# The first pair group of a fused transformer trunk: sums moved into the head, five subtractions moved to GpSimd, gate loads in bursts, stores shifted by a step

## The chip, the cores and the metric

The kernel runs on one core of a Trainium2 chip. TensorE (PE in the profile) multiplies, with a separate sequence of weight loads (PEld); VectorE (DVE), ScalarE (ACT) and GpSimd (POOL) work element by element; SyncE (SP) issues nearly all transfers, in program order. The metric is the device time of one execution in microseconds. Less is better.

## The reference

One decoder layer on 2048 tokens of width 1024, in float32:

```python
mod = silu(c) @ w_ada + b_ada;  shift, scale, gate = split(mod, 3)
u = x * (1 + scale) + shift
q, k, v, a_gate, p_in, p_gate, m_a, m_p = split(u @ w_in, ...)
a = sliding_window_sink_attention(q, k, v, ...) * silu(a_gate) @ w_attn_proj
p = group_linear(multiscale_causal_pool(p_in)) * pool_scale * silu(p_gate) @ w_pool_proj
y = (sigmoid(m_a) * a + sigmoid(m_p) * p) @ w_out * (1 + gate)
x = layer_norm(alpha * x + y)
```

Attention has 16 query heads and 2 key heads of width 64, blocks of 128 and a window of 128.

## The kernel before, in words

**A quad.** The kernel computes large products with a Strassen-like scheme of seven products instead of eight. A `Quad` is two output rows of 128 by two column halves of 512. The moving operands are seven sets (B11, T1, T2, B21, T3, B22, T4), each four tiles of 128x512 in a high and a low part: every float32 operand is split into a rounded high part (a copy on ScalarE) and the rest (a subtraction on VectorE, the helper `low`), and each product runs three matmuls per tile, high x high, high x low, low x high. So one product of a quad with one set is 12 matmuls of 128x512. The weights of a quad go through four stages, F (B11, T1), S (T2, B21), Th (T3, B22) and L (T4), and each stage's weights are sums of loaded quarters: `sum1` and `mid` before F and S, `late` before Th, on GpSimd unless another engine is given. A `w_set` tile in the profile is a split weight, `set_B` and `set_T` the sets, `A` the last quarter. `behind` takes the results out: after T2 it adds the bank of T2's product and a copy of the T1 result (tile `p5`) into the quad's second accumulator, b; the accumulators then go to `consume`.

**The plan.** `plan` orders the products, the splits of weights and the loads of the next quads by steps, one step per product. `run` walks the steps; `at(step, f)` hangs a function on a step, and `defer(n, f)` runs it n steps later. Hooks of a step are emitted behind its product, deferred work behind the hooks. Each engine executes what it is given in this order, and waits only for the data and buffers that the instruction needs: an engine with an empty queue runs an instruction as soon as its inputs exist, whatever step it was written in.

**The first pair group.** The first two quads (keys and values `kv`, and queries `q` 0 and 1) are computed as a pair. Their stages F and S are done in `head`, while x, w_ada and the first weights arrive: `head` loads everything, computes shift and scale on TensorE and VectorE, modulates x, and builds B11, T1, B21, T2 and then T3 as their inputs appear. The arrays `xs` and `ts` hold the modulated input and its differences. B22 is split from `xs[4..7]`, and T4 is `xs[4..7]` minus `ts`. What is left at the end of `head` is hung on steps counted from `base`, the step of the pair's first S product: the late weights of the second quad at step 0, the split of B22 at step 3, T4's differences at step 4, T4's split at step 5. The products still to be run for the pair are, from step 4: T3, B22 of `kv`, T3, B22 of `q`, T4 of `kv`, T4 of `q`; then, at step 10, B11 of the next pair (the gates `ag` and `pg`).

**Work in between.** In the same steps `fold_parts` folds w_pool_mix into the pool's part of w_in: sixteen small products, one per step from step 6, that use the banks pv and pt in turn. Each needs a piece of weights loaded five steps before (`room_raw`, three pieces and one mix matrix), split into `room_w` two steps before, and its result is copied by ScalarE (`st`, in a ring of three tiles of tag x) and stored to `wmix_d`. `gate_modulation` computes the gate: sixteen loads of 128x512 of w_ada into `room_small`, one per step from step 6, each multiplied and summed on VectorE two steps later. `turn_v` transposes value tiles on TensorE through pt and pv, splits them into the second half of `room_small` and stores them. `keep_k` stores key tiles; `q_quad.consume` makes a query tile (`q_hi`, `q_lo`, a ring of four tiles) and stores both parts two steps later.

The steps of the prediction touch lines 235 to 290 (`Quad`), 451 to 475 (`behind`), 546 to 584 (`kv_quad`, `q_quad`), 1170 to 1190 (`gate_modulation`) and 1212 to 1431 (`head` and `first_start`). Every instruction has line 56 in the profile, that of a helper, so groups are told apart by their tiles.

Of the kernel before, what the change touches and what calls it, by code (L numbers as in the profile page):

```python
# [15 lines left out]
ALU = mybir.AluOpType  # L16
# [43 lines left out]
def kernel(  # L60
# [23 lines left out]
    pe, act, dve, pool, sp = (Ordered(tc, e) for e in (nc.tensor, nc.scalar, nc.vector, nc.gpsimd, nc.sync))  # L84
# [9 lines left out]
    def set_tile(n):  # L94
        return cp.tile([P, 4, 2, CH], F32R, tag=f"set_{n}", name=f"set_{n}")

    sets = {n: set_tile(n) for n in ("B11", "T1", "B21")}
# [16 lines left out]
    class SetStore:  # L114
        def __init__(self, name, order=SUM_ORDER):
            self.t = dp.tile([7, 4, P, CH], F32, name=name)
            self.slot = {n: i for i, n in enumerate(order)}
# [15 lines left out]
    q_d = dp.tile([2, KT, 2, 2, P, CH], F32, name="q_d")  # L133
    k_d = dp.tile([2, P, 2, D], F32, name="k_d")
# [6 lines left out]
    def cols(t, n):  # L141
        return t[:, n * CH : (n + 1) * CH]
# [4 lines left out]
    def as32(ap):  # L147
        return ap.bitcast(F32)

    def low(engine, dst, src, hi):  # L150
        engine.tensor_tensor(dst, src, as32(hi), ALU.subtract)

    def mm(*args, **kw):
        pe.matmul(*args, **kw)
# [80 lines left out]
    class Quad:  # L235
        def __init__(self, srcs, consume, sums=None, again=False):
            self.srcs, self.consume, self.sums, self.again = srcs, consume, sums, again
            self.at, self.parts, self.rings, self.opened, self.prefetch = {}, {}, {}, False, None

        def load_w(self, ph, q=sp, a12=True):  # L240
            self.w = x = ph.weights()
            if self.again:
                q.dma_start(x[:, 1:3, :], self.sums)
            else:
                q.dma_start(x[:, 2, :], self.srcs[1][:, 0:CH])
            if a12:
                q.dma_start(x[:, 0::3, :], by_two(self.srcs[0]))
            else:
                q.dma_start(x[:, 0, :], self.srcs[0][:, 0:CH])
# [63 lines left out]
    def defer(ticks, f, local=False):  # L313
        due.append((now[0] + ticks, len(due), f, local))
# [7 lines left out]
    def at(p, f):  # L322
        assert p >= now[0], (p, now[0])
        hooks.setdefault(int(p), []).append(f)
# [126 lines left out]
    def behind(ph, q, kind, h):  # L451
        if kind == "F":
            if h == 0:
                q.c = bank(("lg", "c1")[q.x] if q.pair else "mm")
                if q.x and ph.fresh:
                    t = sets["B11"][:, 0, 0, :]
                    mm(q.c, t[:, 0:P], t, start=True, stop=True, skip_group_check=True)
                    ph.fresh = False
                act.copy(q.c, q.a)
            else:  # L460
                q.p5 = ph.p("p5")
                act.copy(q.p5, q.b)
        elif kind == "S":
            if h == 0:
                dve.tensor_tensor(q.b, q.c, q.p5, ALU.add)
            else:
                q.consume(ph, 0, 0, q.a)
        elif kind == "Th":
            if h == 0:
                dve.tensor_tensor(q.p5, q.c, q.p5, ALU.add)  # L470
                q.consume(ph, 1, 1, q.p5)
            else:
                q.consume(ph, 0, 1, q.b)
        else:
            q.consume(ph, 1, 0, q.c)
# [70 lines left out]
    def kv_quad(s):  # L546
        def keep_k(ph, t, src):
            hi, lo = ph.pair()
            act.copy(hi, src)
            low(dve, lo, src, hi)  # L550
            defer(2, lambda: [sp.dma_start(cols(k_d[s, :, n, :], t), as32(x)) for n, x in enumerate((hi, lo))])

        def turn_v(ph, t, vt):
            vtp = bank(("pv", "pt")[t]).rearrange("p (b a d) -> p b a d", b=NB, a=2)
            for b in range(NB):
                pe.transpose(vtp[:, b].rearrange("p a d -> p (a d)"), vt[:, b * P : (b + 1) * P], ident)
            v = ph.two_halves()
            hi, lo = (v.rearrange("p (a b n d) -> p n b a d", a=2, b=NB, n=2)[:, n] for n in range(2))
            act.copy(hi, vtp)
            low(dve, lo, vtp, hi)  # L560
            v = as32(v).rearrange("p (a b d) -> p a b d", a=2, b=NB)
            defer(2, lambda: [sp.dma_start(v_d[s, :, a, NB * t : NB * (t + 1)], v[:, a]) for a in range(2)])

        def consume(ph, mi, t, src):
            if mi == 0:
                keep_k(ph, t, src)
            else:
                vt = ph.own("vt") if s == 0 else cols(ph.spare(), 0)
                act.activation(vt, src, AF.Copy, scale=0.5)
                defer(2, lambda: turn_v(ph, t, vt))  # L570

        return Quad((win[TK], win[TV]), consume)

    def q_quad(s, m):
        def consume(ph, mi, t, src):
            hi, lo = ph.c("q_hi", F32R), ph.c("q_lo", F32R)
            act.activation(hi, src, AF.Copy, scale=-0.125)
            dve.scalar_tensor_tensor(lo, src, -0.125, as32(hi), ALU.mult, ALU.subtract)
            defer(2, lambda: [sp.dma_start(q_d[s, m + mi, t, n], as32(x)) for n, x in enumerate((hi, lo))])

        kept = (sums_d[1 + m // 2], s == 1) if m else ()
        return Quad((win[TQ + m], win[TQ + m + 1]), consume, *kept)
# [517 lines left out]
    rooms = {}  # L1100
# [69 lines left out]
    def gate_modulation(base):  # L1170

        def room(j):
            return cols(rooms["small"], j % 2)

        def fetch(j):
            sp.dma_start(room(j), cols(wada[2 * KT + j // 2], j % 2))

        def work(j):
            m = mod[:, 2 * KT + j // 2 : 2 * KT + j // 2 + 1]
            w = room(j)  # L1180
            dve.tensor_tensor_reduce(w, w, cols(rooms["cb"], j % 2), 1.0, m, ALU.mult, ALU.add, m)

        def gate_row():
            dve.tensor_scalar(mod[:, 2 * KT :], mod[:, 2 * KT :], 0.5, None, ALU.mult)

        for j in range(2 * KT):
            p = base + 6 + j
            at(p, lambda j=j: fetch(j))
            at(p + 2, lambda j=j: work(j))
        at(base + 24, gate_row)  # L1190
# [21 lines left out]
    def head(ph, grp):  # L1212
# [6 lines left out]
        small = ph.t.tile([P, 2 * D], F32, tag="small", bufs=1, name="head_small")  # L1219
# [21 lines left out]
        xs, ts, sums, starts = {}, {}, {}, []  # L1241
# [33 lines left out]
        def minus(dst, a, b):  # L1275
            dve.tensor_tensor(dst, a, b, ALU.subtract)

        def parts(name, i, src):
            split_set(name, i, src, (act, dve))
# [30 lines left out]
        opened = [[bank(), bank(), None, None] for q in grp]  # L1310
# [80 lines left out]
        sets["T3"] = set_tile("T3")  # L1391
        for i in range(4):
            parts("T3", i, xs[i][0])
        third = [ph.split(False) for _ in range(2)]
        act.copy(by_two(third[0]), grp[0].third())
        low(dve, by_two(third[1]), grp[0].third(), by_two(third[0]))
        grp[0].parts["Th"] = third

        def t4_sums():
            for i in range(4):  # L1400
                minus(xs[4 + i][0], xs[4 + i][0], ts[i])
            sets["T4"] = set_tile("T4")

        def late_parts(name, c):
            return lambda: [parts(name, i, xs[4 + i][c]) for i in range(4)]

        sets["B22"] = set_tile("B22")
        dve.tensor_scalar(nsink, nsink, -1.0, None, ALU.mult)
        rest = (0, lambda: grp[1].late(dve)), (3, late_parts("B22", 1)), (4, t4_sums), (5, late_parts("T4", 0))
        for q, o in zip(grp, opened):  # L1410
            q.a, q.b, q.c, _, q.p5 = o
            q.opened = True
        return rest

    def first_start(ph, phase):
        rest = head(ph, phase["groups"][0])
        base = phase["base"]
        rooms["raw"] = ph.t.tile([P, 2 * D], F32, tag="big", bufs=1, name="room_raw")
        rooms["w"] = ph.t.tile([P, 2 * D], F32R, tag="big2", bufs=1, name="room_w")

        def small_room():
            rooms["small"] = ph.t.tile([P, 2 * D], F32, tag="small", bufs=1, name="room_small")

        ph.turns["v"] = cycle([lambda: cols2(rooms["small"], 1).bitcast(F32R)])
        for n, f in rest:
            at(base + n, f)
        at(base + 5, small_room)
        for j in range(2):
            at(base + 10 + j, lambda j=j: spread_bias(j, act))
        fold_parts(ph, base)  # L1430
        gate_modulation(base)
# [73 lines left out]
    parts = []  # L1505
# [61 lines left out]
```

## Time and profile before

| | |
|---|---|
| time, median of 3 runs | 1728.42 us (1728.2 to 1731.76) |
| the profiled execution: time, span, mean granted clock | 1734.96 us, 1732.8 us, 0.986 |
| busy PE, DVE, ACT, POOL | 1675.2, 1273.3, 945.2, 588.6 us |
| chain that ended last | PE 68%, DVE 11%, DMA 8%, ACT 7%, issue 5% |
| DMA | 389.50 MB, 225 GB/s |

A time below is in microseconds from the start of the span. In the timeline each row is a start, a duration, the engine, the operation with its output and inputs, and in brackets how long the engine had been idle before and what ended that. `SPq` is SyncE's issue of a transfer; its duration is the time the issue took, with waiting. `xN` stands for N instructions merged into a row.

### The profile page before, as it was taken

What the parts mean: (1) busy time and instruction counts of PE and PEld (TensorE: products, weight loads), DVE (VectorE), ACT (ScalarE), POOL (GpSimd) and SP (SyncE); (2) the same over time, 40 slices, a digit from 0 to 9 for tenths busy, and PEclk for the clock granted to TensorE, in tenths of its full rate; (3) what the DMA queues carried; (4) which work ended last, traced back from release to release, by engine and by line L of the source; (5) the groups of instructions that cost most, each with busy time, mean ns of one, the idle gap of its engine ahead of it and who ended that gap; (6) DMA issues with size and microseconds to landing.
All of it is one profiled execution on the core that took longest, in us unless ns stands there. A gap on an engine that the chain in (4) does not pass through costs nothing.

```text
span 1732.8 us, 24858 instructions
## 1 busy us (share of the span) xinstructions
PE 1675.2 (97%) x8112; PEld 1399.7 (81%) x8112; DVE 1273.3 (73%) x2296; ACT 945.2 (55%) x1815; POOL 588.6 (34%) x562
## 2 busy tenths in 40 slices
PE   9889999999999999999999999999999999999996
PEld 7678788878788888888888888888788888888775
DVE  5846787768757778558787887587877785877667
ACT  3644777667753445457767677334544343435442
POOL 3012455545453223323424333322232211124443
PEclk8999999989999999999999999999999999999998
DMA  9389666766556788864446453689968786785432
GB/s 352 123 280 295 216 221 223 253 211 192 186 174 218 258 284 307 296 223 150 152 167 211 152 187 124 199 282 310 341 212 292 237 316 215 239 292 200 146 146 109
DMA packets 236545, 389.50 MB, mean 225 GB/s; under 512 B 20840, under 2 KB 90240, under 8 KB 236288
## 3 DMA queue, kind: packets, MB, share of 16 engines
q1 hardware_dynamic: 235344, 386.55, 66.4%
q8 instruction: 64, 1.05, 0.3%
q10 hardware_dynamic: 1040, 1.34, 0.2%
q14 instruction: 65, 0.53, 0.1%
q0 software_dynamic: 32, 0.02, 0.0%
HBM read 243.63 MB, written 147.35 MB: 226 GB/s over the span
## 4 chain that ended last, share of the span: by engine, by line
PE 68%; DVE 11%; DMA 8%; ACT 7%; issue 5%; SPq 1%; POOL 0%; DVEq 0%; ACTq 0%; POOLq 0%
PE mm L56 42%; PE lg L56 11%; PE c L56 9%; DVE w_set L56 3%; PE pv L56 3%; PE pt L56 3%; DVE wide L56 2%; DVE L L56 2%; ACT L L56 2%; ACT w_set L56 2%; SPq L56 1%; DMA q_d<-q_hi 1%; ACT sig L56 1%; DMA out_dram<-wide 1%; DMA bt<-e_rep 1%
## 5 line engine op out<-in xcount | busy, mean ns | idle before, releaser
L56 PE MATMUL mm<-set_B,w_set 128*128 128x512 f32 x2664 | 656.0, 393 | 1.4 <-DVE w_set L56 1.2
L56 PEld LDWEIGHTS mm<-set_B,w_set 128*128 128x128 f32 x2664 | 499.5, 189 | 104.9 <-DVE w_set L56 1.7
L56 POOL TENSOR_TENSOR W<-W 128x512 f32<-128x512 f32 x185 | 270.0, 1469 | 579.4 <-DVE w_set L56 380.1
L56 PE MATMUL mm<-set_T,w_set 128*128 128x512 f32 x1824 | 453.1, 396 | 0.5 <-DVE set_T L56 0.5
L56 PEld LDWEIGHTS mm<-set_T,w_set 128*128 128x128 f32 x1824 | 341.2, 190 | 70.6 <-DVE set_T L56 1.6
L56 DVE TENSOR_TENSOR w_set<-W,w_set 128x1024 fp32r<-128x1024 f32 x198 | 256.1, 1294 | 121.1 <-ACT w_set L56 111.2
L56 ACT CAST w_set<-W 128x1024 fp32r<-128x1024 f32 x222 | 232.2, 1047 | 85.4 <-PE mm L56 48.8
L56 ACT ACTIVATE L<-L 128x257 f32<-128x257 f32 (+3 forms) x384 | 191.2, 500 | 117.9 <-DVE L L56 117.2
L56 PE MATMUL c<-set_T,w_set 128*128 128x512 f32 x864 | 212.5, 394 | 5.5 <-ACT w_set L56 3.0
L56 PE MATMUL lg<-set_T,w_set 128*128 128x512 f32 x864 | 211.0, 392 | 4.8 <-DVE mm L56 1.6
L56 PEld LDWEIGHTS c<-set_T,w_set 128*128 128x128 f32 x864 | 162.8, 190 | 42.0 <-ACT w_set L56 4.2
L56 PEld LDWEIGHTS lg<-set_T,w_set 128*128 128x128 f32 x864 | 161.6, 188 | 41.7 <-DVE set_T L56 2.8
L56 POOL TENSOR_TENSOR W<-W,A 128x512 f32<-128x512 f32 x41 | 56.0, 1365 | 275.5 <-DMA A<-in_win_dram 130.5
L56 DVE CUSTOM_DVE_ANT_0 L<-lg,bt,nsink 128x256 f32<-128x256 f32 (+1 forms) x256 | 111.0, 470 | 23.3 <-PE lg L56 16.8
L56 DVE TENSOR_TENSOR ptl<-pt,pth 128x512 fp32r<-128x512 f32 (+1 forms) x128 | 85.8, 670 | 29.9 <-ACT pth L56 29.0
L56 PEld LDWEIGHTS lg<-kk,qs 128*128 128x128 f32 x512 | 76.5, 190 | 37.1 <-DVE L L56 27.0
L56 PE MATMUL lg<-kk,qs 128*128 128x256 f32 (+1 forms) x512 | 83.6, 286 | 18.6 <-DVE L L56 18.5
L56 DVE TENSOR_SCALAR L<-L 128x256 f32<-128x256 f32 (+1 forms) x128 | 96.6, 755 | 4.5
L56 ACT ACTIVATE sig<-mm 128x512 f32<-128x512 f32 x76 | 45.5, 598 | 96.9 <-PE mm L56 94.7
L56 ACT CAST pth<-pt 128x512 fp32r<-128x512 f32 (+1 forms) x128 | 72.2, 564 | 23.8 <-PE pv L56 23.0
L56 PE MATMUL pv<-pth,vv 128*128 128x256 f32 x248 | 75.6, 326 | 2.1 <-DMA vv<-v_d 2.1
L56 POOL TENSOR_TENSOR w_set<-W,w_set 128x1024 fp32r<-128x1024 f32 x24 | 58.1, 2422 | 56.8 <-ACT w_set L56 29.0
(208 smaller groups left out, 1949.3 us busy)
## 6 DMA issues: line engine op xcount, KB each, us to landing
W<-in_win_dram SPq DMA_DIRECT2D x40, 512.0 KB, 6.1
qs<-q_d SPq DMA_DIRECT2D x128, 128.0 KB, 4.4
sums_d<-W SPq DMA_DIRECT2D x62, 256.0 KB, 4.2
W<-sums_d SPq DMA_DIRECT2D x31, 512.0 KB, 3.8
ain_d<-st SPq DMA_DIRECT2D x56, 256.0 KB, 3.8
A<-in_win_dram SPq DMA_DIRECT2D x42, 256.0 KB, 5.4
q_d<-q_hi SPq DMA_DIRECT2D x32, 256.0 KB, 3.9
q_d<-q_lo SPq DMA_DIRECT2D x32, 256.0 KB, 4.1
```

What stands on the lines that cost most here:

```text
L56: return lambda *args, **kw: self.tc.keep_in_program_order(op(*args, **kw))
```

## The change

- The sum behind T2 (`q.b = q.c + q.p5`) of both quads of the first pair is emitted in `head`, the first quad's ahead of the low half of its third weights, the second's behind it. A flag `summed` keeps `behind` from doing it again.
- The first two of B22's four tiles are split in `head`, behind T3's split; the other two stay at step 3.
- The late weights of the second quad (step 0) and T4's four differences (step 4) are emitted for GpSimd instead of VectorE. T4's split moves from step 5 to step 6, and with it the new use of `room_small`.
- Gate loads: four rooms instead of two, from step 12 with eight loads in five steps, instead of one per step from step 6. The works stay two steps behind their loads; the last load stays at step 21.
- Stores: the first key tiles three steps behind instead of two; the query tiles of the first query quad (of both chunks of the sequence) one step instead of two; the first value turning of the first chunk three steps instead of two.

```diff
+            self.summed = False
...
         elif kind == "S":
             if h == 0:
-                dve.tensor_tensor(q.b, q.c, q.p5, ALU.add)
+                if not q.summed:
+                    dve.tensor_tensor(q.b, q.c, q.p5, ALU.add)
...
-            defer(2, lambda: [sp.dma_start(cols(k_d[s, :, n, :], t), as32(x)) for n, x in enumerate((hi, lo))])
+            defer(2 if t else 3, lambda: [sp.dma_start(cols(k_d[s, :, n, :], t), as32(x)) for n, x in enumerate((hi, lo))])
...
-                defer(2, lambda: turn_v(ph, t, vt))
+                defer(2 if s else 2 + t, lambda: turn_v(ph, t, vt))
...
-            defer(2, lambda: [sp.dma_start(q_d[s, m + mi, t, n], as32(x)) for n, x in enumerate((hi, lo))])
+            defer(2 if m else 1, lambda: [sp.dma_start(q_d[s, m + mi, t, n], as32(x)) for n, x in enumerate((hi, lo))])
...
-            return cols(rooms["small"], j % 2)
+            return cols(rooms["small"], j % 4)
...
-            p = base + 6 + j
+            p = base + 12 + 5 * j // 8
             at(p, lambda j=j: fetch(j))
             at(p + 2, lambda j=j: work(j))
...
         for i in range(4):
             parts("T3", i, xs[i][0])
+        sets["B22"] = set_tile("B22")
+
+        def late_parts(name, c, ks):
+            return lambda: [parts(name, i, xs[4 + i][c]) for i in ks]
+
+        late_parts("B22", 1, (0, 1))()
+        for q, o in zip(grp, opened):
+            q.a, q.b, q.c, _, q.p5 = o
+            q.opened = q.summed = True
+        dve.tensor_tensor(grp[0].b, grp[0].c, grp[0].p5, ALU.add)
         third = [ph.split(False) for _ in range(2)]
         act.copy(by_two(third[0]), grp[0].third())
         low(dve, by_two(third[1]), grp[0].third(), by_two(third[0]))
         grp[0].parts["Th"] = third
+        dve.tensor_tensor(grp[1].b, grp[1].c, grp[1].p5, ALU.add)
 
         def t4_sums():
             for i in range(4):
-                minus(xs[4 + i][0], xs[4 + i][0], ts[i])
+                pool.tensor_tensor(xs[4 + i][0], xs[4 + i][0], ts[i], ALU.subtract)
             sets["T4"] = set_tile("T4")
...
-        rest = (0, lambda: grp[1].late(dve)), (3, late_parts("B22", 1)), (4, t4_sums), (5, late_parts("T4", 0))
...
+        rest = (
+            (0, grp[1].late),
+            (3, late_parts("B22", 1, (2, 3))),
+            (4, t4_sums),
+            (6, late_parts("T4", 0, range(4))),
+        )
...
-        at(base + 5, small_room)
+        at(base + 6, small_room)
```

More of the change, by code (lines that the diff above doesn't have):

```diff
@@ L1397, in head @@
         grp[0].parts["Th"] = third
+        dve.tensor_tensor(grp[1].b, grp[1].c, grp[1].p5, ALU.add)
         def t4_sums():
             for i in range(4):
-                minus(xs[4 + i][0], xs[4 + i][0], ts[i])
+                pool.tensor_tensor(xs[4 + i][0], xs[4 + i][0], ts[i], ALU.subtract)
             sets["T4"] = set_tile("T4")
-        def late_parts(name, c):
-            return lambda: [parts(name, i, xs[4 + i][c]) for i in range(4)]
-        sets["B22"] = set_tile("B22")
         dve.tensor_scalar(nsink, nsink, -1.0, None, ALU.mult)
-        rest = (0, lambda: grp[1].late(dve)), (3, late_parts("B22", 1)), (4, t4_sums), (5, late_parts("T4", 0))
-        for q, o in zip(grp, opened):
-            q.a, q.b, q.c, _, q.p5 = o
-            q.opened = True
+        rest = (
[4 more added lines that the diff above has]
+        )
         return rest
```

## The prediction

> **What bounds the kernel now.** I read the page's busy shares first, then busy time by stretches of the head and of the first pair group, TensorE's waits there, and the timeline.
>
> ```profile
> PE 1675.2 (97%) x8112; PEld 1399.7 (81%) x8112; DVE 1273.3 (73%) x2296; ACT 945.2 (55%) x1815; POOL 588.6 (34%) x562
> ...
> 51.00:64.00 13.00, 11.64 (x37) 8.62 (x38) 12.43 (x20) 7.83 (x15) 0.00 (x0) 0.74 0.12 42
> 64.00:82.00 18.00, 12.35 (x59) 9.41 (x58) 16.95 (x27) 11.05 (x19) 2.37 (x1) 1.00 0.54 163
> 82.00:94.80 12.80, 12.79 (x75) 11.10 (x73) 7.43 (x11) 6.01 (x10) 3.85 (x3) 1.00 0.94 319
> 94.80:104.65 9.85, 5.49 (x18) 4.53 (x19) 4.39 (x7) 3.75 (x6) 1.21 (x1) 0.65 0.76 262
> 104.65:110.00 5.35, 5.35 (x36) 4.85 (x36) 1.36 (x3) 2.91 (x5) 1.33 (x2) 1.00 0.83 240
> ```
>
> The columns after the stretch's length are busy PE, PEld, DVE, ACT, POOL, then granted clock, DMA share and GB/s. TensorE is the bound of the whole (97%), so only its holes can be won. It lacks 18.00 - 12.35 = 5.65 us in the second stretch, where VectorE is busy 16.95 of 18.00, and 9.85 - 5.49 = 4.36 us in the fourth, where the clock also falls to 0.65. After 104.65 it has none. So I carry the sum to 104.65, the end of the second group's first product, and take what is won there as won at the end.
>
> ```profile
> PE pv L56 <- ACT st L56: 4.4, 1, 4.4
> PE pv L56 <- DVE spare L56: 1.6, 1, 1.6
> PE lg L56 <- DVE mm L56: 1.6, 1, 1.6
> PE pt L56 <- ACT vt L56: 1.5, 1, 1.5
> PE pv L56 <- ACT spare L56: 1.0, 1, 1.0
> ```
>
> These five are all of TensorE's waits from 64 to 105 us: 10.1 us. The change aims at 1.6 (sum), 1.5 (turned values), 4.4 (a copy).
>
> **The 4.4 us wait and the query stores.**
>
> ```profile
> 70.36 6.71 SPq L56 DMA_DIRECT2D room_raw<-in_wpt_dram  x2
> 77.11 0.60 SPq L56 DMA_DIRECT2D q_d<-q_hi  x1
> 90.11 0.51 SPq L56 DMA_DIRECT2D q_d<-q_hi  x1
> 92.45 0.61 SPq L56 DMA_DIRECT2D wmix_d<-st  x1
> 96.06 0.60 ACT L56 ACTIVATE q_hi<-c 128x512 fp32r<-128x512 f32 x1 [4.90 <-DMA q_d<-q_hi]
> 98.53 0.59 ACT L56 COPY st<-pv 128x512 f32<-128x512 f32 x1 [1.87 <-DMA wmix_d<-st]
> 99.93 4.72 PE L56 MATMUL mm<-set_B,w_set 128*128 128x512 f32 x12
> 105.91 2.91 PE L56 MATMUL mm<-set_T,w_set 128*128 128x512 f32 x12
> ```
>
> SP issues in order. Its second folding load waits 6.71 us for a VectorE split, and the first query store queues behind it. The query store of 90.11 has queued behind two folding loads and two gate loads; ScalarE's fourth query tile waits 4.90 us for it to free a buffer, and the copy that empties bank pv, behind it, then waits until 98.5 for the folded weights' store of 92.45. Only then does TensorE turn the last values, and the cold product takes 4.72 instead of 2.91 us. The wait and the clock cost 4.37 + 1.81 = 6.2 us.
>
> Edit: the four query tiles of the first quad go out one step sooner, that is ahead of the next step's loads; gate loads start at step 12 instead of 6 and leave the queue free. In the new order of the queue the store that frees the fourth tile's buffer issues behind the folding load whose split ends near 87.7 (below) and the two key stores, about 89, and lands some 5 us later (90.11 to 96.06 is 5.95), before the fourth tile needs it (97.5, when T4's second product ends). The folded weights' store follows the next folding load, whose split ends near 90.6, and three issues of some 0.6 us: it stays near 92.5 and the copy is free near 98.5 as now. If the query wait stayed, 4.9 us would come back.
>
> **GpSimd: late weights and T4's differences.** Five subtractions of 128x512 leave VectorE (0.60 us from start to start, 3.0 us in all) for GpSimd.
>
> ```profile
> 51.17 1.23 DVE L56 TENSOR_TENSOR w_set<-W,w_set 128x1024 fp32r<-128x1024 f32 x1 [1.26 <-ACT w_set L56]
> 52.31 1.28 DVE L56 CUSTOM_DVE_ANT_0 head_big<-head_big,cb,mod 128x1024 f32<-128x1024 f32 x1
> 54.85 0.69 DVE L56 TENSOR_TENSOR set_T<-head_T,set_T 128x512 fp32r<-128x512 f32 x1
> 57.04 0.68 DVE L56 TENSOR_TENSOR set_B<-head_small,set_B 128x512 fp32r<-128x512 f32 x1
> 75.28 2.37 POOL L56 TENSOR_TENSOR W<-W,A 128x512 f32<-128x512 f32 x1 [51.98 <-DMA A<-in_win_dram]
> 103.44 2.54 POOL L56 TENSOR_TENSOR W<-W 128x512 f32<-128x512 f32 x2 [11.58 <-DVE w_set L56]
> 1253.00 2.32 DVE L56 TENSOR_TENSOR w_set<-W,w_set 128x1024 fp32r<-128x1024 f32 x1
> 1252.03 8.91 POOL L56 TENSOR_TENSOR W<-W 128x512 f32<-128x512 f32 x4 [6.34 <-DVE w_set L56]
> ```
>
> One takes 2.54/2 = 1.27 us on GpSimd. The point is when. GpSimd is idle for 52 us until 75.28, and its queue holds these five next. The late weights' last reader on VectorE ends at 51.17 + 1.23 = 52.4; the last of the differences' inputs is through at 57.04 + 0.68 = 57.7. So GpSimd does not wait for the step where they are written: it starts at 52.4, in the middle of the stretch where VectorE is busy 12.43 of 13.00.
>
> And the two block each other where both read two operands in SBUF. At 1252 four GpSimd subtractions take 8.91 us instead of 4 x 1.27, and VectorE's low half, 1.23 alone at 51.17, takes 2.32: they take turns, each operation waiting out the other. VectorE's operations from 52.3 to 64 are of this kind. Bounds: five turns of 1.25 us lost, 6.2, less 0.5 of VectorE's own gaps, so 5.7; or nothing, if GpSimd gets no turn among short back-to-back operations (at 75.28 its 1.08 us of extra time let one more VectorE operation pass first). I take 5.7, the row with four turns. Three of the five fall before the set_T of 54.85, whose end moves from 55.5 to some 59.1 (3.6 later); TensorE waits for it and then works 9.9 us as now (55.6 to 65.5, where its 1.60 us wait for 67.11 begins), to 69.0. The Trainium skill, "SBUF — State Buffer", section "Who interferes with whom", has the shared pair as an exclusive lock in which issue order decides who blocks; by that GpSimd is not starved, and the sum stays at its high bound.
>
> **Sums in the head and late_parts.**
>
> ```profile
> 62.63 1.29 DVE L56 TENSOR_TENSOR set_T<-x,set_T 128x512 fp32r<-128x512 f32 x2
> 65.05 1.23 DVE L56 TENSOR_TENSOR w_set<-W,w_set 128x1024 fp32r<-128x1024 f32 x1 [1.13 <-ACT w_set L56]
> 66.27 0.69 DVE L56 TENSOR_TENSOR mm<-lg,p 128x512 f32<-128x512 f32 x1
> 67.11 2.98 PE L56 MATMUL lg<-set_T,w_set 128*128 128x512 f32 x12 [1.60 <-DVE mm L56]
> 69.26 1.29 DVE L56 TENSOR_TENSOR set_B<-A,set_B 128x512 fp32r<-128x512 f32 x2
> 72.80 0.69 DVE L56 TENSOR_TENSOR p<-lg,p 128x512 f32<-128x512 f32 x1
> 74.30 0.63 PE L56 MATMUL pt<-ident,vt 128*128 128x128 f32 x4 [1.46 <-ACT vt L56]
> 80.68 1.58 PE L56 MATMUL pv<-spare,room_w 128*128 128x256 f32 x11 [1.60 <-DVE spare L56]
> 81.14 0.68 DVE L56 TENSOR_TENSOR room_small<-pt,room_small 128x512 fp32r<-128x512 f32 x1
> 86.28 2.91 PE L56 MATMUL lg<-set_T,w_set 128*128 128x512 f32 x12
> ```
>
> Step by step, old time -> new time:
> - VectorE ends T3's low halves: 63.9 -> 63.9 + 5.7 = 69.6.
> - Now two of B22's low halves come first (1.2, filling the 1.13 that VectorE idles before 65.05), then the sum (0.7), so T3's product starts at 71.5 instead of 67.11. Without port waits it would be 65.85: this part alone is worth 1.26 us. Its third weight matrix needs the low half that now follows the sum (1.2), so it ends near 75.0 instead of 69.9; B22's product near 77.9 instead of 72.8.
> - The turning of the values moves behind the next product: the 1.46 us wait goes. That product starts at 77.9 instead of 74.7, ends at 80.8.
> - The first folding needs its operands split. From the sum's end VectorE has 9 operations of 0.6 and 2 of 1.14 before that (the late weights and differences are gone from the list), 1.3 us of waiting for ScalarE, and up to one turn of 1.25 lost to the GpSimd sum now at 75.28: 71.3 + 9.1 = 80.4 to 81.6, taken as 81.3. It ends at 82.9 (1.58), the transposes (0.5) at 83.4. The next product starts there instead of at 82.1.
> - What is late next: the second folding writes bank pt, which the turned values leave only after VectorE's room_small operation (81.14 now, 5 us ahead of T4's product at 86.28). Ahead of it now stand, from 81.6, three operations of 0.6, 0.7 for ScalarE, one more, T4's four low halves (2.4) and a split: it ends near 88.4 and the folding, which could start at 86.3, waits 2.1 us. T4's first product starts at 90.1 instead of 86.3.
> - From there to the end of the fourth folding 8.5 us as now: 98.6 instead of 94.8. The copy is ready by then; the transposes and the warm product end near 102.7 instead of 104.65.
>
> Sum: +4.4 (T3's start) +0.6 -1.5 -2.2 (folding waits) +2.5 (bank pt, transposes in line) -6.2 +0.4 (the copy) = -2.0 us.
>
> One term hangs on the clock: TensorE stands some 2.5 us before T3's product (69.0 to 71.5). I charge nothing: the 1.6 us wait before 67.11 left the clock at 1.00, the 4.4 us wait did not. The Trainium skill, "TensorE: Matmul & The Clock Gate", section "What's actually happening", gives half clock after one idle window of about 3.4 us; by it 2.5 us costs nothing either, while the row of the 4.4 us wait alone would allow up to 1.8.
>
> **Gate loads and the second chunk.**
>
> ```profile
> v_d<-room_small SPq DMA_DIRECT2D x4, 256.0 KB, 5.9
> ```
>
> Sixteen loads now fall into ten steps instead of sixteen, in four rooms of which two are also the values' room: the third load must wait for the values' store (5.9 us to land, one or two steps of 4.2 us before), so SP stands up to 1.7 us, with a folding load and a folded weights' store behind it. Cover: after 104.65 TensorE has no hole, and each copy has a whole product (2.9 us) before its bank is wanted. Zero; without the cover 1.7. The first key stores, a step later, let the next gate weights' loads pass; these wait for the third low half of the first quad (72.5) anyway, and the GpSimd sum they feed is off the path. In the second chunk the same edits shift a queue that waits for the same data: zero, or a step's 0.6 us of issue either way.
>
> **Rivals.**
> (a) GpSimd gets no turn until VectorE's first gap. Then T3 starts at 65.85, everything up to bank pt comes 5.7 earlier, and the store of the folded weights too: -7.7, 1720.7. For: the turn lost at 75.28; against: four turns taken at 1252.
> (b) The gain is given back after 105 by fuller DMA queues (0.76 to 0.94 busy already): 1728.4. Against: TensorE full there.
> (c) Slower: the hole that the port waits cut into TensorE, up to 59.1, keeps its clock at half up to T3.
>
> ```profile
> 58.10 1.28 PE c L56 x3
> ...
> 60.75 0.68 PE mm L56 x3
> ```
>
> These pieces of the chain of waits give a matmul 1.28/3 = 0.43 us cold and 0.23 warm. 27 matmuls more at 0.43 end at 74.5 rather than 69, so T3 starts 3.0 us later, and with B22 runs 20 of its matmuls cold, 4.0 more: -2 + 7 = +5, 1733.4. It decides if the clock is not back by about 64. For: 0.74 in the stretch of 51 to 64 now. Against: now it is back by 60.75, some 5 us after TensorE goes on.
> (d) The query stores are not freed, as above: +4.9 - 2 = +2.9, 1731.3.
>
> **How the numbers follow.** The profiled execution took 1734.96 us (span 1732.8), 6.5 more than the median of 1728.42; a difference in the head carries over, so I put it to the median: 1728.42 - 2.0 = 1726.4. Chances: forecast 0.43, (a) or half of it 0.32, (b) 0.10, (c) 0.10, (d) 0.05. Own range of the forecast: 1723 to 1729. For all: 1718.5 to 1732. 0.2% is 3.5 us, what a measurement of this kernel can tell from no change: (a) lies beyond it, and a quarter of the forecast's own spread, so faster 0.42; slower (c), part of (d) and unforeseen 0.16; within 0.42.
>
> **What would show it.** Right: five GpSimd subtractions between 52 and 64, VectorE operations of 1.2 to 1.9 us there, T3's product at 71 to 72, the first query store before 76, no DMA wait above 1 us on q_hi, the product after the last turning in 2.9 us, a wait for bank pt before the second folding. Wrong: T3 before 68 (then a), or matmuls of 0.4 us after 63 (then c), or new holes after 105 (then b).

## The result, and the profile after

The changed kernel takes 1731.53 us (median; 1728.77 to 1739.11), the kernel before, run beside it, 1728.56 us. The ratio is 1.0023 with a 95% interval of 1.0014 to 1.0033: slower by 4.0 us (2.4 to 5.7); the two medians lie 3.0 us apart. The forecast was 1726.4. The profiled execution took 1739.11 us, span 1737.3, clock 0.985; it is the slowest of its 20, so single durations in it are compared with other kernels' profiles below.

Busy time of the changed kernel in the first four of the prediction's stretches (length, then busy PE, PEld, DVE, ACT, POOL, granted clock, DMA share, GB/s):

```profile
PE 1678.6 (97%) x8112; PEld 1401.6 (81%) x8112; DVE 1279.3 (74%) x2291; ACT 945.6 (54%) x1815; POOL 595.7 (34%) x567
...
51.00:64.00 13.00, 10.00 (x32) 7.51 (x31) 12.91 (x15) 4.78 (x9) 8.64 (x5) 0.77 0.00 1
64.00:82.00 18.00, 14.27 (x57) 10.72 (x56) 13.83 (x22) 9.48 (x16) 1.30 (x1) 0.91 0.54 170
82.00:94.80 12.80, 9.50 (x58) 8.15 (x57) 9.31 (x13) 7.95 (x14) 3.03 (x2) 1.00 0.66 232
94.80:104.65 9.85, 9.13 (x54) 7.59 (x53) 5.07 (x6) 5.38 (x9) 1.32 (x2) 1.00 0.78 274
```

Everything up to 51 runs some 2 us earlier here than in the profile of before (51.17 there is 49.21 here), so the stretches don't hold quite the same work. GpSimd now works 8.64 us between 51 and 64, where it did nothing, and VectorE, busy 12.91 of 13.00, gets 15 operations through instead of 20. The fourth stretch is nearly full at full clock (9.13 against 5.49), but new holes stand in the third (9.50 against 12.79), and the second has lost part of its clock (0.91).

GpSimd's and then VectorE's timeline in the head:

```profile
50.52 2.25 POOL L56 TENSOR_TENSOR W<-W 128x512 f32<-128x512 f32 x1 [28.49 <-DMA room_raw<-in_mix_dram]
52.74 3.38 POOL L56 TENSOR_TENSOR x<-x,head_T 128x512 f32<-128x512 f32 x2
56.08 1.72 POOL L56 TENSOR_TENSOR head_small<-head_small,head_T 128x512 f32<-128x512 f32 x1
59.69 1.84 POOL L56 TENSOR_TENSOR head_small<-head_small,head_T 128x512 f32<-128x512 f32 x1 [1.89 <-DVE set_B L56]
```

```profile
49.21 1.22 DVE L56 TENSOR_TENSOR w_set<-W,w_set 128x1024 fp32r<-128x1024 f32 x1 [1.26 <-ACT w_set L56]
...
51.62 1.70 DVE L56 SCALAR_TENSOR_TENSOR head_T<-head_T,sg,head_small 128x512 f32<-128x512 f32 x1
53.24 1.75 DVE L56 TENSOR_TENSOR set_B<-head_small,set_B 128x512 fp32r<-128x512 f32 x1
54.92 3.42 DVE L56 TENSOR_TENSOR set_T<-head_T,set_T 128x512 fp32r<-128x512 f32 x2
...
60.31 2.38 DVE L56 TENSOR_TENSOR spare<-head_T,spare 128x512 f32<-128x512 f32 x2
...
68.03 0.69 DVE L56 TENSOR_TENSOR mm<-lg,p 128x512 f32<-128x512 f32 x1
```

These are the five subtractions, written at steps 0 and 4 and run in the head. The four VectorE operations from 51.62 to 58.3 take 1.7 us each instead of 0.7, the two from 60.31 take 2.38 together instead of 1.29. TensorE's timeline and its waits from 40 to 110 us:

```profile
56.72 1.04 PE L56 MATMUL lg<-set_T,w_set 128*128 128x512 f32 x2 [3.00 <-DVE set_T L56]
...
68.86 0.70 PE L56 MATMUL lg<-set_T,w_set 128*128 128x512 f32 x2 [2.32 <-DVE mm L56]
69.90 4.05 PE L56 MATMUL lg<-set_T,w_set 128*128 128x512 f32 x10 [0.33 <-DVE w_set L56]
...
89.05 1.69 PE L56 MATMUL pt<-spare,room_w 128*128 128x256 f32 x12 [3.30 <-DVE room_small L56]
...
99.94 3.00 PE L56 MATMUL mm<-set_B,w_set 128*128 128x512 f32 x12
...
104.76 2.91 PE L56 MATMUL mm<-set_T,w_set 128*128 128x512 f32 x12
```

```profile
PE pt L56 <- DVE room_small L56: 3.3, 1, 3.3
PE lg L56 <- DVE set_T L56: 3.2, 2, 3.0
PE lg L56 <- DVE mm L56: 2.3, 1, 2.3
...
PE pv L56 <- ACT st L56: 0.4, 1, 0.4
```

The wait that the change aimed at (the copy of bank pv, `ACT st`, 4.4 us) has shrunk to 0.4. In its place stand 3.0 us for a late `set_T`, 2.3 for the sum, and 3.3 for bank pt.

**A common ruler.** The low half `w_set<-W,w_set` of 49.21, the second quad's S weights, comes before everything that is changed. It starts between 46.6 and 53.3 us in the executions profiled here, so all times below count from it. "T3" is the start of T3's first product, "stretch" the time to the second product of the gates' pair (104.76 here): 104.76 - 49.21 = 55.55. A dash in the table of the next section is a wait below 0.3 us. In the profile of before T3 and the stretch are 67.11 - 51.17 = 15.94 and 105.91 - 51.17 = 54.74.

On this ruler the copy that empties bank pv starts at 98.89 - 49.21 = 49.68, in the profile of before at 98.53 - 51.17 = 47.36. So the copy didn't come sooner: its wait shrank because TensorE itself came later.

### The profile page after: what moved, and what is told of

It reads as the page before. It is cut to its first block, busy times and chain, and to the rows that moved or that the text cites. A ratio compares the mean times of both kernels' runs of the same rounds, so it can differ in the third digit from the quotient of the medians.

```text
span 1737.3 us, 24857 instructions
## 1 busy us (share of the span) xinstructions
PE 1678.6 (97%) x8112; PEld 1401.6 (81%) x8112; DVE 1279.3 (74%) x2291; ACT 945.6 (54%) x1815; POOL 595.7 (34%) x567
## 4 chain that ended last, share of the span: by engine, by line
PE 71%; DVE 12%; ACT 6%; DMA 5%; issue 5%; SPq 0%; POOL 0%; DVEq 0%; ACTq 0%
PE mm L56 44%; PE lg L56 12%; PE c L56 9%; PE pv L56 3%; PE pt L56 3%; DVE w_set L56 3%; DVE wide L56 2%; DVE L L56 2%; ACT L L56 2%; ACT w_set L56 1%; DMA q_d<-q_hi 1%; DVE set_T L56 1%; ACT sig L56 1%; DVE p L56 1%; DMA bt<-e_rep 1%
```

## The experiments

Each ratio is to the kernel before, run beside that kernel. T3, the stretch and the waits are of one execution each; the two profiles of before differ by 1.3 us in the stretch, so a smaller difference in it says nothing by itself.

| kernel | ratio to before (95%) | T3 | stretch | wait `ACT st` | wait for bank pt |
|---|---|---|---|---|---|
| before, first profile | 1 | 15.94 | 54.74 | 4.4 | - |
| before, again | | 15.62 | 53.42 | 2.3 | - |
| after | 1.0023 [1.0014, 1.0033] | 19.65 | 55.55 | 0.4 | 3.3 |
| pool_only | 1.0017 [1.0004, 1.0029] | 19.66 | 55.45 | 2.0 | - |
| no_pool | 0.9981 [0.9968, 0.9994] | 14.71 | 48.65 | 0.4 | 2.2 |
| late_only | 1.0009 [0.9996, 1.0022] | 16.23 | 50.11 | 0.8 | 0.6 |
| held | 1.0015 [1.0001, 1.0028] | 15.34 | 53.85 | - | 3.8 |
| turn_first | 1.0026 [1.0014, 1.0038] | 19.65 | 57.14 | 3.8 | - |
| split_late | 0.9988 [0.9974, 1.0001] | 14.70 | 48.25 | - | - |
| gates_stores | 1.0009 [0.9993, 1.0025] | 14.72 | 52.45 | 2.1 | - |
| stores_only | 1.0024 [1.0012, 1.0035] | 14.72 | 54.39 | 4.3 | - |
| no_pool_gates_early | 0.9994 [0.9979, 1.0010] | 14.70 | 51.37 | 2.2 | 0.7 |
| sums_only | 0.9989 [0.9976, 1.0001] | 14.71 | 50.79 | 0.9 | 2.2 |
| sums_gates | 0.9975 [0.9964, 0.9986] | 14.72 | 47.92 | - | 2.2 |

### The five subtractions: alone, and taken back

pool_only is the kernel before with them on GpSimd; no_pool is the changed kernel with them on VectorE.

```diff
# pool_only
-                minus(xs[4 + i][0], xs[4 + i][0], ts[i])
+                pool.tensor_tensor(xs[4 + i][0], xs[4 + i][0], ts[i], ALU.subtract)
...
-        rest = (0, lambda: grp[1].late(dve)), (3, late_parts("B22", 1)), (4, t4_sums), (5, late_parts("T4", 0))
+        rest = (0, grp[1].late), (3, late_parts("B22", 1)), (4, t4_sums), (5, late_parts("T4", 0))
```

> The kernel before with one part of the change alone: the late weights of the second quad and T4's four differences on GpSimd, where they were written. Port theory (the five operations run at once and take turns with VectorE): five GpSimd subtractions between 50 and 62 us, T3's first product 4 to 5 us later than before, and of this 1 to 3 us left at the end, 1729.5 to 1731.5 for a kernel before of 1728.5. Rival (the loss of the change comes after 105 us, from the gate loads or the stores): T3 within 1 us of before, end time the same within 1 us.

> The changed kernel with these five subtractions back on VectorE, all else as changed. Port theory: T3's product starts some 5 us earlier than in the changed kernel, VectorE has 3.0 us more work behind it, and 2 to 3 us of gain are left: about 1729. Rival (loss after 105 us): 1731 to 1732 as the changed kernel.

pool_only alone is slower than before, 1.0017, and has T3 at 19.66 as the changed kernel has. no_pool is faster than before, 0.9981 (1724.39 us, where I expected about 1729). TensorE's timeline in no_pool, and VectorE's sum there:

```profile
63.94 0.70 PE L56 MATMUL lg<-set_T,w_set 128*128 128x512 f32 x2 [0.48 <-DVE mm L56]
64.97 2.57 PE L56 MATMUL lg<-set_T,w_set 128*128 128x512 f32 x10 [0.33 <-DVE w_set L56]
...
82.17 1.70 PE L56 MATMUL pt<-spare,room_w 128*128 128x256 f32 x12 [2.22 <-DVE room_small L56]
...
97.88 2.91 PE L56 MATMUL mm<-set_T,w_set 128*128 128x512 f32 x12
```

```profile
49.23 1.23 DVE L56 TENSOR_TENSOR w_set<-W,w_set 128x1024 fp32r<-128x1024 f32 x1 [1.26 <-ACT w_set L56]
...
63.09 0.70 DVE L56 TENSOR_TENSOR mm<-lg,p 128x512 f32<-128x512 f32 x1
```

This and the changed kernel start the ruler within 0.02 us of each other, so the two traces can be laid over one another. The sum comes at 63.09 instead of 68.03: 4.94 us. Ten matmuls of T3's product take 2.57 instead of 4.05: 1.48. The wait for bank pt is 2.22 instead of 3.30: 1.08. Those are 7.5; the stretch differs by 55.55 - 48.65 = 6.9, and the times by 1.0023 / 0.9981 = 1.0042 (7.3 us; the two intervals together leave an estimated 4.5 to 10). The five subtractions on GpSimd are the whole loss, and the rest of the change is a gain. Alone, in pool_only, they cost 2.9 us (0.7 to 5.0). At T3 they cost 3.7 to 4.0 us there, against 4.9 beside the other edits; the rest of that difference isn't explained.

### One of the five alone

```diff
# late_only: the changed kernel, T4's differences on VectorE
-                pool.tensor_tensor(xs[4 + i][0], xs[4 + i][0], ts[i], ALU.subtract)
+                minus(xs[4 + i][0], xs[4 + i][0], ts[i])
```

> The changed kernel with T4's four differences back on VectorE; only the late weights' subtraction of the second quad stays on GpSimd. Theory (each GpSimd subtraction that meets VectorE in the head costs about one turn): one turn only, about 1.3 us of the 5, so T3's product starts 15.5 to 16.3 us after the low half of the third weights, and the time is about 1.5 us above the kernel without any GpSimd subtraction: ratio 0.9988 to 1.000 (1726.5 to 1728.5). Rival (the late weights alone open the hole, since they are the first to collide and delay set_T): T3 at 18 us or later and ratio above 1.001.

T3 comes at 16.23, 1.5 us behind no_pool, and the stretch is 1.5 longer. That isn't one turn on VectorE, though: its sum starts at 61.12 - 46.62 = 14.50 on the ruler, against 63.09 - 49.23 = 13.86 in no_pool, 0.64 later (with all five it is 18.82, 4.96 later). The rest is TensorE, which runs three matmuls in 1.49 us up to 56.9, 10.2 on the ruler, and isn't through with the product ahead of T3 when the sum is ready. The kernel `held` below has the same one subtraction in the head, its sum at 14.50 too, and T3 at 15.34. The time is above what I expected of it (1.0009, where 1.000 was the upper end), but its interval reaches down to 0.9996; that it costs more than its turn isn't shown.

### The differences held back

```diff
# held: the changed kernel, T4's differences behind the GpSimd sum of step 5
-            (4, t4_sums),
+            (5, t4_sums),
```

> The changed kernel with one edit: T4's four differences stay on GpSimd but are written one step later, behind the sum of the next weights, which waits for its own load until some 77 us; GpSimd is in order, so they can't run in the head. Port theory: only the late weights take a turn there, T3's product starts 3 to 4 us earlier than in the changed kernel, and the time falls by 4 to 6 us against it, to 1725 to 1727. Rival (GpSimd subtractions are the cost wherever they run, 1.27 against 0.60 us each): within 1.5 us of the changed kernel.

On GpSimd the differences now stand behind a sum whose input arrives at 69.5. GpSimd's and VectorE's timeline in held:

```profile
69.47 1.39 POOL L56 TENSOR_TENSOR W<-W,A 128x512 f32<-128x512 f32 x1 [19.23 <-DMA A<-in_win_dram]
70.82 2.49 POOL L56 TENSOR_TENSOR x<-x,head_T 128x512 f32<-128x512 f32 x2
73.28 3.41 POOL L56 TENSOR_TENSOR head_small<-head_small,head_T 128x512 f32<-128x512 f32 x2
```

```profile
72.12 1.74 DVE L56 TENSOR_TENSOR spare<-room_raw,spare 128x512 fp32r<-128x512 f32 x1 [1.81 <-ACT spare L56]
73.78 1.76 DVE L56 TENSOR_TENSOR room_w<-room_raw,room_w 128x512 fp32r<-128x512 f32 x1
75.47 1.76 DVE L56 TENSOR_TENSOR w_set<-A,w_set 128x512 fp32r<-128x512 f32 x1
```

T3 is back at 15.34, yet the kernel stays slower than before (1.0015, where I expected 1725 to 1727 us), with the longest wait for bank pt of all, 3.8 us. The differences meet VectorE here too: the three operations shown take 1.75 us instead of 0.69, and T4's split and bank pt's operation stand behind them. By the time, the rival that the GpSimd subtractions cost wherever they run isn't refuted: 1.0015 is 1.4 us from the changed kernel's 1.0023.

### Is it bank pt?

```diff
# turn_first: the changed kernel, value turning and T4's split where they were
-                defer(2 if s else 2 + t, lambda: turn_v(ph, t, vt))
+                defer(2, lambda: turn_v(ph, t, vt))
...
-            (6, late_parts("T4", 0, range(4))),
+            (5, late_parts("T4", 0, range(4))),
...
-        at(base + 6, small_room)
+        at(base + 5, small_room)
# split_late: no_pool, T4's split in two halves
-            (6, late_parts("T4", 0, range(4))),
+            (6, late_parts("T4", 0, (2, 3))),
+            (7, late_parts("T4", 0, (0, 1))),
```

> The changed kernel with the first turning of values at two steps again, ahead of the product, and with T4's split back at step 5. Bank theory (the 3.3 us wait of the second folding for bank pt comes from the turned values standing behind T4's four low halves): that wait falls below 1 us, a wait of about 1.5 us for the turned values returns, and the time falls by 1 to 2 us against the changed kernel, to about 1730. Rival (VectorE's list is the limit there, whatever its order): the wait moves to the next folding and the time stays at 1731.5.

> The changed kernel with the five subtractions on VectorE, and two of T4's four splits a step later, behind the operation that empties bank pt. Bank theory: the second folding's wait (2.2 us in the kernel with the subtractions on VectorE) falls to about 1, and the time with it by 1 us, to 1723. Rival: the T4 product waits for its splits instead, 1724.5.

Both take the wait for bank pt away, and neither is faster for it. In turn_first the gain of 3.3 us goes to the next wait, the copy of bank pv, and to the cold product behind it:

```profile
98.14 1.11 PE L56 MATMUL pv<-ident,vt 128*128 128x128 f32 x4 [3.77 <-ACT st L56]
98.91 5.17 PE L56 MATMUL mm<-set_B,w_set 128*128 128x512 f32 x12
```

In split_late the stretch shortens by 0.4 us only: the wait for a split of folding operands (`ACT spare`) is 1.8 us instead of 1.5, and eleven matmuls behind it take 2.72 instead of 1.58. Its interval and no_pool's overlap. So in these two kernels the wait for bank pt is a place where delays show: a hole closed at pt opens elsewhere, in turn_first at pv.

### What removes the 4.4 us wait: stores, loads or sums

before_again is the kernel before itself, profiled a second time.

```diff
# gates_stores: the kernel before with these; stores_only: with the first two
...
+            defer(2 if t else 3, lambda: [sp.dma_start(cols(k_d[s, :, n, :], t), as32(x)) for n, x in enumerate((hi, lo))])
...
+            defer(2 if m else 1, lambda: [sp.dma_start(q_d[s, m + mi, t, n], as32(x)) for n, x in enumerate((hi, lo))])
...
+            return cols(rooms["small"], j % 4)
...
+            p = base + 12 + 5 * j // 8
# no_pool_gates_early: no_pool with the last two as before
# sums_gates: no_pool with the first two as before; sums_only: with all four as before
```

> The kernel before, a second profile of it. From the low half of the second quad's S weights on VectorE (the last thing before the GpSimd operations may start) to the second product of the gates' pair it took 54.7 us in the first profile. If that profile is typical, within 1 us of it again; if it was an unlucky one (its execution was 6.5 us above the median), 50 to 53.

> The kernel before with the key and query stores and the gate loads as changed, nothing else. Queue theory: the fourth query tile no longer waits for its buffer, the 4.4 us wait of TensorE and the cold product after it shrink by 3 to 6 us in all: 1723 to 1726. Rival (given back later: the gate loads in bursts fill the DMA queues between 110 and 180 us): 1728 to 1730, with new waits of TensorE after 105 us.

> The kernel before with only the key and query stores shifted, gate loads as before. Theory (these stores alone do not free the copy of bank pv, because it waits for the folded weights' store behind the queue of gate loads): the wait for the copy that holds bank pv stays at 2 us or more, the stretch is 53.5 to 54.5, ratio 0.9995 to 1.0008. Rival (the query store sets it, as the prediction said): wait under 1 us, stretch 51 to 52, ratio 0.9982 to 0.999.

> The changed kernel with the five subtractions on VectorE and the gate loads as before (two rooms, one per step from step 6). Queue theory: the gate loads stand in the queue ahead of the query and folded weights' stores, the copy that frees bank pv comes 2 to 4 us later, and the time rises by 2 to 4 us to 1726.5 to 1728.5. Rival (the burst of gate loads costs later what the free queue wins): 1723 to 1725.

> The kernel before with the head's edits alone: both sums and two tiles of B22's split in the head, T4's split a step later, the first value turning a step later. Late weights and T4's differences on VectorE, gate loads and stores as before. Theory (the gain of the change sits in these edits; the loads and stores are worth 2 to 3 us in the head and lose about half of it later): T3's product starts 14.7 us after the low half of the third weights, the stretch to T4's gates product (second product of the gates' pair) is 51.4 to 52.5 instead of about 54, and the time is 1.5 to 2.5 us under before (ratio 0.9985 to 0.9992). Rival (the gain needs all edits together): a wait for bank pv or for a query buffer of 4 us or more takes it back, stretch 54 or more, ratio 1.000.

> The changed kernel with all five subtractions on VectorE and the key and query stores back where they were before: it keeps the sums in the head, the two tiles of B22's split, the later value turning and the later gate loads. Theory (the copy that empties bank pv waits for the folded weights' store; shifted stores stand ahead of it in the queue, so they gain nothing and may cost): the wait for that copy stays under 1 us without them, T3 at 14.7 after the low half of the third weights, stretch to the gates' second product 48 to 49.5, time 3 to 5 us under before (ratio 0.997 to 0.9985). Rival (the shifted query stores are what frees the fourth query tile): a wait of 2 us or more for that copy, with a cold product behind it, stretch 51 or more, ratio 0.999 to 1.000.

TensorE's waits in the second profile of before:

```profile
PE pv L56 <- ACT st L56: 2.3, 1, 2.3
PE pv L56 <- DVE spare L56: 1.6, 1, 1.6
PE lg L56 <- DVE mm L56: 1.6, 1, 1.6
PE pt L56 <- ACT vt L56: 1.5, 1, 1.5
PE pv L56 <- ACT spare L56: 1.0, 1, 1.0
```

Four of the five waits are as in the first profile; the one that the prediction's largest term rests on is 2.3 instead of 4.4. TensorE's timeline there:

```profile
78.16 4.51 PE L56 MATMUL mm<-set_B,w_set 128*128 128x512 f32 x12
...
94.71 0.67 PE L56 MATMUL pv<-ident,vt 128*128 128x128 f32 x4 [2.27 <-ACT st L56]
95.13 4.59 PE L56 MATMUL mm<-set_B,w_set 128*128 128x512 f32 x12
```

The product behind the copy is cold (on a lowered clock) here as well, and so is the one behind the first folding, which took 2.91 us in the first profile. So the stretch, 53.42, is only 1.3 shorter: neither within the 1 us that would have called the first profile typical, nor below 53.

gates_stores, from which I expected 1723 to 1726 us, is at 1.0009: the copy's wait only halves, to 2.1. ScalarE and SP show which transfer it is that the copy waits for. stores_only first, then sums_gates:

```profile
91.36 0.62 SPq L56 DMA_DIRECT2D wmix_d<-st  x1
...
91.62 0.60 ACT L56 ACTIVATE q_hi<-c 128x512 fp32r<-128x512 f32 x1 [2.25 <-PE c L56]
96.65 0.59 ACT L56 COPY st<-pv 128x512 f32<-128x512 f32 x1 [4.43 <-DMA wmix_d<-st]
```

```profile
83.21 0.60 SPq L56 DMA_DIRECT2D q_d<-q_hi  x1
84.85 0.63 SPq L56 DMA_DIRECT2D wmix_d<-st  x1
...
88.30 0.60 ACT L56 ACTIVATE q_hi<-c 128x512 fp32r<-128x512 f32 x1 [2.25 <-PE c L56]
89.03 0.59 ACT L56 COPY st<-pv 128x512 f32<-128x512 f32 x1
```

With the stores moved alone, the fourth query tile waits for no transfer any more, only for its product (2.25 of `PE c`), and TensorE still stands 4.3 us for the copy: it waits for the folded weights' store, which is issued at 91.36, behind the stores that were moved ahead of it, and whose buffer is free at 96.65. In sums_gates the stores are where they were, and both waits are gone: the sums in the head and the later loads let SP issue that store at 84.85, which is 37.6 on the ruler against 42.2 in stores_only. The sums with the later turning do most of it: in sums_only, with loads and stores as before, the wait is 0.9. So the query store, whose shift the prediction made the condition of its largest term, was not the one that closed last.

By the times, the sums with B22's two tiles and the later turning are worth 1.9 us (0.9989, interval up to 1.0001); with the later gate loads 4.3 us (0.9975, interval 2.4 to 6.2); with the shifted stores on top it is 3.3 (0.9981). With the gate loads early again, no_pool_gates_early has the copy's wait back at 2.2 and a ratio of 0.9994, as expected, though its interval overlaps no_pool's. A gain from the shifted stores doesn't show there, and alone they are slower than before (1.0024). sums_gates, 1724.52 us against 1728.86, has the lowest ratio and is faster than both the kernel before and the changed one; its interval overlaps those of no_pool, split_late and sums_only, so which of these is best isn't shown.

stores_only's stretch is not longer than before's first (54.39 against 54.74), so its 4 us are lost somewhere behind; where is open. The same holds in small for the others: no_pool's stretch is 4.8 to 6.1 us shorter than the two of before, its time only 3.3 us (1.0 to 5.5). Of that 1.7 us show in TensorE's waits: from 105 to 320 it waits 5.0 us instead of 3.9 for `DVE L` and 0.6 for the query tiles' loads, which it didn't before.

## Why the prediction was wrong

**What came as said.** Five GpSimd subtractions between 50.5 and 61.5; VectorE operations of 1.7 us beside them; T3 at 19.65 on the ruler, where 71.5 - 51.17 = 20.3 was forecast; the query store at 73.25, ahead of 76; no transfer waited for at the fourth query tile; the product behind the last turning in 3.00 us; the wait for bank pt ahead of the second folding. Rival (a), that GpSimd gets no turn, fell: T3 at 14.7 is what no_pool shows, and pool_only is 5 us from it. The Trainium skill, "SBUF — State Buffer", section "Who interferes with whom", has GpSimd's and VectorE's shared ports as an exclusive lock; the trace agrees, with 9.19 us for five subtractions (2.25 + 3.38 + 1.72 + 1.84) that take 1.27 each alone, 6.4 in all, and VectorE's 1.7 instead of 0.7 beside them.

**Which steps failed.** Three terms of the sum were mis-sized. The table sets the terms of the sum beside what TensorE's timeline shows, as differences of the starts of these products between after and each profile of before.

| part of the sum | forecast | against the first profile | against the second |
|---|---|---|---|
| T3's start | +4.4 | +3.7 | +4.0 |
| T3's product | +0.6 | +2.1 | +2.1 |
| from its end to the second folding (-1.5 -2.2 +2.5) | -1.2 | +0.4 | -1.2 |
| from there to the fourth folding | 0 | +0.1 | +0.1 |
| the copy and the product behind it (-6.2 +0.4) | -5.8 | -5.5 | -2.9 |
| in all | -2.0 | +0.8 | +2.1 |

**The clock of T3's product was put at nothing**, and this misses against both profiles. After 2.32 us of waiting, ten of its matmuls took 4.05 us instead of 2.57, which is 1.5 us. It happened again in turn_first (2.31 us, then 4.15). It need not happen: after 1.92 us in pool_only the product took 2.98. So the size of this term is in part luck.

**The wait for bank pt was sized too small**, 2.1 us where it was 3.3. GpSimd and VectorE met once more, over T4's last two low halves, which took 2.36 us instead of 1.29 in no_pool, where the wait is 2.22:

```profile
85.24 1.81 POOL L56 TENSOR_TENSOR W<-W,A 128x512 f32<-128x512 f32 x1 [7.16 <-DMA A<-in_win_dram]
```

```profile
85.24 2.36 DVE L56 TENSOR_TENSOR set_T<-head_small,set_T 128x512 fp32r<-128x512 f32 x2
```

Against the second profile this doesn't show in the table, because the cold product of 78.16 there makes up for it.

**The term -6.2 was carried over whole.** It was read from one execution, which the same part called 6.5 us above the median, and then put to the median. Against that execution the last part of the sum held (-5.5 of -5.8). In the second profile the wait is 2.27 and the product 4.59 instead of 2.91, so the term would have been 2.3 + 1.7 = 4.0 there, and of -5.8 only -2.9 came.

**The 1.26 us credited to the sums at T3's start** depend on the execution. Both profiles of before have T3 later than no_pool's 14.71, by 1.23 and 0.91 us. There ScalarE's copy of the third weights waited 1.79 and 1.48 us for TensorE. In gates_stores and stores_only, with the sum where it was before, it didn't wait, and T3 comes at 14.72. The GpSimd turns cost T3 19.65 - 14.71 = 4.9 us, of which the comparison of after with before shows only 3.7.

**What stays open.** The stretch explains +0.8 to +2.1 of the +4.0 (2.4 to 5.7). What is left lies after 105, as rival (b) had it, in part: TensorE waits there for 0.5 us of query loads and 0.9 us more for `DVE L`. How much more is lost, these profiles can't tell, since the granted clock differs there between executions of one kernel: summed over pieces of 20 us after 105, one minus the granted clock is 12.3 us in the first profile of before, 9.0 in the second, 15.7 in after. Rival (c), the clock at half up to T3, is refuted as said (TensorE was at 0.84 us for three matmuls from 61.6 on), but a loss of clock of its kind appeared one product later.

## What to carry to other kernels

An operation handed to an idle engine runs when its inputs are ready, not at the step where it is written; if the two engines slow each other down, as here, count that for every meeting, also after moving it: held only changed where they met. Size a wait from more than one execution before it becomes the largest term of a sum, above all where a transfer's landing ends it: the copy of bank pv came 6.1 us after the issue of the store that it waited for in one profile of before (92.45 to 98.53), 4.1 in the other (90.02 to 94.08). Of a bundle of edits, each one undone alone tells more than the bundle: here the version with the lowest ratio leaves out the subtractions on GpSimd and the shifted stores.

## What was new of the hardware

The clock after a short hole isn't settled by the hole's length. gates_stores and stores_only have the same head up to T3 and both wait 2.07 us for the sum (TensorE's timeline, gates_stores first):

```profile
67.98 4.25 PE L56 MATMUL lg<-set_T,w_set 128*128 128x512 f32 x12 [2.07 <-DVE mm L56]
```

```profile
63.88 2.97 PE L56 MATMUL lg<-set_T,w_set 128*128 128x512 f32 x12 [2.07 <-DVE mm L56]
```

The same twelve matmuls take 4.25 us in one, at a granted clock of 0.67, and 2.97 in the other, at 1.00. The same at 182 us, after waits of 1.87 us in after and 1.98 in before: fifteen matmuls in 5.13 against 3.59 us (after first).

```profile
183.36 5.13 PE L56 MATMUL mm<-set_T,w_set 128*128 128x512 f32 x15
```

```profile
184.03 3.59 PE L56 MATMUL mm<-set_T,w_set 128*128 128x512 f32 x15
```

The Trainium skill, "TensorE: Matmul & The Clock Gate", section "What's actually happening", has half clock after an idle window of about 3.4 us, and the window running free of the kernel. These holes are shorter and did lose the clock, so the length it gives is not a safe bound; that two equal holes go different ways fits a free-running window, which no run here shows by itself.
